# Down projection of a gated hybrid block: difference forms built in the convolution and kept in HBM, six plain groups first, 24 instead of 22 seven-product groups

## The chip, the core and the metric

The kernel runs on one core of a Trainium2 chip. The metric is the device time of one execution in microseconds (us): the median of three runs is 1472.03 us before the change (1471.71, 1472.03 and 1474.16). TensorE (PE) does the matmuls; VectorE (DVE) and ScalarE (ACT) prepare their operands; GpSimd (POOL) and SyncE (SP) here do little but issue DMA transfers.

## The reference

The function is one decoder layer for 256 tokens of width 2048: three kinds of attention, gated and merged, and then a feed-forward part. The change touches only the feed-forward part, which is

```python
h2 = rms_norm(x, g_ffn[l])
u = causal_depthwise_conv(h2 @ w_up[l], conv_w[l], conv_b[l])   # 3 taps, 2 x 5632 channels
u_gate, u_val = jnp.split(u, 2, axis=-1)
x = x + (jax.nn.silu(u_gate) * u_val) @ w_down[l]               # 5632 x 2048
```

Everything is float32 and must come out as precisely as float32 does. The kernel therefore splits every operand into a rounded high part (`hi`, a cast on ACT) and the remainder (`lo`, a subtraction on DVE), and makes three matmuls (hi by hi, lo by hi, hi by lo) where the reference has one product.

## The kernel before, in words

Two stages matter. In the **up projection** (748 to 1241 us of the profiled execution) 11 groups of four column tiles are worked through, each in two halves: the gate columns (`s = 0`) and the value columns (`s = 1`). One half takes eight *ticks*. A tick takes one 512 KB piece of `w_up` (`piece`: load on SP, cast L175 on ACT, subtraction L176 on DVE) and 16 matmuls (eight hi at L1219, eight lo at L1221). The result of a half goes through `conv`, a generator whose pieces are run by `tick()` during the following halves, so its DVE and ACT work is interleaved with the casts and subtractions of the next ticks. After the `s = 1` half, `conv` writes the activation's high and low part for one pair of row tiles into `aT`.

Beside this run the *weight sums* (`weight_sums`, one every seven ticks): the second GEMM uses a Winograd-like scheme in some of its groups, seven block products in place of eight, and needs sums of blocks of `w_down`. Four blocks are loaded into `r0` (one buffer) and `r1` (two buffers) by SP, three or four DVE additions (L1181) make the sums, and POOL stores them to HBM as `T`: one half-megabyte tile (T4 and T2), and a second one (T1 and T3) where four additions were made (`ALL_FOUR`).

The **down projection** (1241 to 1466 us) has 44 groups: 22 pairs of row tiles of `w_down` for each half of the 2048 output columns. `PLANS` sets their order. A plain group (`eight`, "e") has two steps of 12 matmuls. A seven group (`seven`, "s") has four steps of 3, 6, 6 and 6 matmuls, 21 in all; it uses sums of weight blocks against *forms*, that is sums and differences of blocks of the activation. Each step has a preparation, written into the program two steps ahead of its matmuls (`AHEAD = 2`): a load through `buffer`, a ring of four `raw` buffers and, every third turn, two `more` buffers; a cast; a subtraction. The cast and the subtraction write into rings of four `hi` and four `lo` buffers (`SBUFS = 4`). In the seven group, step 0 loads the first row tile, step 1 the second, step 2 the sums T4 and T2, step 3 either loads T1 and T3 or makes them by two DVE additions into a buffer of its own, `t13` (L1371, L1372).

The forms of a pair are made in the down projection by `forms(p)`: five DVE operations on `aT` (L1273 to L1277), two casts on ACT and two subtractions on DVE (L1284, L1285), all in one `fr` buffer.

Every engine, SP included, takes its instructions in program order; `keep` pins that order. A load whose buffer is still being read makes SP wait, and whatever stands behind it in SP's queue waits as well.

## Time and profile before

| what | value | how to read it |
|---|---|---|
| time, median of 3 | 1472.03 us (1471.71 to 1474.16) | device time of a run |
| profiled execution, span | 1469.9 us | first to last instruction; 1.8 us below the fastest run |
| PE busy | 1462.8 us (100%) | the share is rounded; 7.1 us are left |
| DVE / ACT busy | 1205.1 us (82%) / 895.3 us (61%) | |
| up projection, PE / DVE busy | 492.5 / 394.7 of 493.2 us | stage from 748.0 to 1241.2 us |
| down projection, PE / DVE / ACT busy | 224.4 / 208.6 / 140.9 of 224.5 us | stage from 1241.2 to 1465.7 us |
| HBM | 349.70 MB read, 37.75 MB written | |

A row of a timeline reads: start, duration, engine, line, operation, destination<-sources, shapes, and in brackets the idle time ahead of it with what ended it. A row of waits reads: who waited for whom, total, number of waits, longest. The granted TensorE clock is 1.00 in all three stretches of the span (0 to 748, up projection, down projection).

### The profile page before, as it was taken

The numbers are of one execution on the slowest core, as the hardware profiler recorded it, in microseconds if no ns is written. First come the engines' busy times: TensorE is split into PE (matmuls) and PEld (weight loads), VectorE is DVE, ScalarE is ACT, GpSimd is POOL, SyncE is SP. The second block draws the span as 40 slices with busy tenths as digits, with TensorE's granted clock in tenths as the row PEclk, the third lists the DMA queues.
The fourth block names the chain that finished last, engine by engine and source line by source line (L and its number), as shares of the span: only waits on it lengthen the run. The fifth ranks groups of instructions, "written<-read, shape, count | busy, mean of one in ns | idle before, by whom it ended". The sixth has DMA issues, their size and how long they took to land.

```text
span 1469.9 us, 20741 instructions
## 1 busy us (share of the span) xinstructions
PE 1462.8 (100%) x7327; PEld 1233.4 (84%) x7327; DVE 1205.1 (82%) x1617; ACT 895.3 (61%) x1287; POOL 68.8 (5%) x139
## 2 busy tenths in 40 slices
PE   9999999999999999999999999999999999999998
PEld 7888888888878888888888888888888888888887
DVE  5798767766997799888877888788887886998998
ACT  6755454454664466545657667567676777665774
POOL 1000001021000000000000000000000010000000
PEclk9999999999999999999999999999999999999999
DMA  8697898787766576866776888889888895778995
GB/s 295 202 341 260 265 313 270 226 294 267 256 221 204 204 271 247 287 222 237 273 239 218 302 272 276 294 277 310 295 265 273 280 305 190 249 256 286 334 315 191
DMA packets 163463, 388.81 MB, mean 265 GB/s; under 512 B 14016, under 2 KB 22512, under 8 KB 163360
## 3 DMA queue, kind: packets, MB, share of 16 engines
q1 hardware_dynamic: 150960, 345.34, 70.6%
q0 software_dynamic: 11648, 41.10, 7.3%
q8 instruction: 57, 0.93, 0.3%
q10 hardware_dynamic: 752, 1.06, 0.2%
q14 instruction: 46, 0.38, 0.1%
HBM read 349.70 MB, written 37.75 MB: 264 GB/s over the span
## 4 chain that ended last, share of the span: by engine, by line
PE 94%; DVE 3%; DMA 2%; issue 1%; ACT 0%; SPq 0%; DVEq 0%; ACTq 0%
PE u L1219 21%; PE u L1221 10%; PE d L1310 5%; PE d L1309 5%; PE d L1311 5%; PE g_x L769 4%; PE g_x L770 4%; PE g_x L771 4%; PE s L186 2%; PE s L188 2%; PE f L187 2%; PE f L188 2%; PE f L186 2%; PE s L187 2%; PE b L186 2%; PE b L188 2%
## 5 line engine op out<-in xcount | busy, mean ns | idle before, releaser
L1219 PE MATMUL u<-hT,hi_u 128*128 128x512 f32 x1408 | 442.6, 396 | 0.0
L1221 PEld LDWEIGHTS u<-hT,lo_u 128*128 128x128 f32 x1408 | 264.4, 188 | 63.5 <-DVE lo_u L176 1.1
L1221 PE MATMUL u<-hT,lo_u 128*128 128x256 f32 x1408 | 277.0, 278 | 0.7 <-DVE lo_u L176 0.7
L176 DVE TENSOR_TENSOR lo_u<-raw_u,hi_u 128x1024 fp32r<-128x1024 f32 x176 | 213.2, 1220 | 59.8 <-ACT hi_u L175 59.0
L175 ACT CAST hi_u<-raw_u 128x1024 fp32r<-128x1024 f32 x176 | 183.0, 1049 | 107.0 <-PE u L1219 54.6
L1219 PEld LDWEIGHTS u<-hT,hi_u 128*128 128x128 f32 x1408 | 214.5, 189 | 0.1
L764 ACT CAST hi_g<-raw_g 128x1024 fp32r<-128x1024 f32 (+1 forms) x96 | 91.1, 964 | 53.5 <-PE g_x L770 33.4
L765 DVE TENSOR_TENSOR lo_g<-raw_g,hi_g 128x1024 fp32r<-128x1024 f32 (+1 forms) x96 | 105.0, 1116 | 20.9 <-ACT hi_g L764 20.8
L769 PE MATMUL g_x<-hi_g,xT 128*128 128x512 f32 x251 | 98.8, 394 | 0.0
L770 PE MATMUL g_x<-hi_g,xT 128*128 128x512 f32 x251 | 97.7, 389 | 0.0
L771 PE MATMUL g_x<-lo_g,xT 128*128 128x512 f32 x251 | 96.3, 390 | 0.0
L1148 DVE TENSOR_TENSOR y<-y,z 128x512 f32<-128x512 f32 x88 | 60.7, 691 | 24.4 <-ACT z L1147 20.5
L1147 ACT ACTIVATE z<-u,taps 128x256 f32<-128x256 f32 x176 | 74.7, 496 | 0.0
L1309 PE MATMUL d<-hi_d,aT 128*128 128x512 f32 x176 | 68.5, 389 | 0.0
L1310 PE MATMUL d<-hi_d,aT 128*128 128x512 f32 x176 | 68.5, 389 | 0.0
L1311 PE MATMUL d<-lo_d,aT 128*128 128x512 f32 x176 | 68.1, 389 | 0.0
L175 ACT CAST hi_f<-raw_f 128x1024 fp32r<-128x1024 f32 (+1 forms) x40 | 38.6, 968 | 46.6 <-PE f L187 41.9
L186 PE MATMUL s<-hi_s,xT 128*128 128x512 f32 (+1 forms) x160 | 61.9, 387 | 0.0
L175 ACT CAST hi_b<-raw_b 128x1024 fp32r<-128x1024 f32 x32 | 33.6, 1052 | 45.2 <-PE b L187 23.5
L175 ACT CAST hi_s<-raw_s 128x1024 fp32r<-128x1024 f32 (+1 forms) x40 | 38.3, 959 | 36.8 <-PE s L187 29.3
L186 PE MATMUL f<-hi_f,xT 128*128 128x512 f32 (+1 forms) x160 | 60.4, 377 | 0.0
L188 PE MATMUL s<-lo_s,xT 128*128 128x512 f32 (+1 forms) x160 | 59.1, 369 | 0.0
(498 smaller groups left out, 3265.0 us busy)
## 6 DMA issues: line engine op xcount, KB each, us to landing
raw_u<-in_w_up_dram SPq DMA_DIRECT2D x176, 512.0 KB, 5.4
raw_g<-in_w_in_dram SPq DMA_DIRECT2D x86, 512.0 KB, 5.4
T<-r POOLq DMA_DIRECT2D x64, 512.0 KB, 6.1
r<-in_w_down_dram SPq DMA_DIRECT2D x88, 256.0 KB, 5.2
raw_d<-in_w_down_dram SPq DMA_DIRECT2D x44, 512.0 KB, 5.4
raw_f<-in_w_in_dram SPq DMA_DIRECT2D x32, 512.0 KB, 5.5
raw_s<-in_w_in_dram SPq DMA_DIRECT2D x32, 512.0 KB, 5.4
raw_s<-in_w_down_dram SPq DMA_DIRECT2D x32, 512.0 KB, 5.3
```

The lines of the kernel that those rows point to most:

```text
L175: pin(nc.scalar.copy(hi[:, :m], raw[:, :m]))
L176: pin(nc.vector.tensor_tensor(lo[:, :m], raw[:, :m], hi[:, :m].bitcast(F32), ALU.subtract))
L186: nc.tensor.matmul(o, lhsT=xh, rhs=wh, start=first, stop=False)
L188: nc.tensor.matmul(o, lhsT=xh, rhs=wl, start=False, stop=last)
L769: nc.tensor.matmul(o, lhsT=a[0], rhs=w[0], start=first, stop=False)
L770: nc.tensor.matmul(o, lhsT=a[1], rhs=w[0], start=False, stop=False)
L771: nc.tensor.matmul(o, lhsT=a[0], rhs=w[1], start=False, stop=last)
L1219: nc.tensor.matmul(ps, lhsT=hi[:, j, c], rhs=hT[:, k + j, :], start=first, stop=False)
L1221: nc.tensor.matmul(ps[:, :S], lhsT=lo[:, j, c], rhs=hT[:, k + j, :S], start=False, stop=last)
L1309: nc.tensor.matmul(o, lhsT=ah, rhs=w[0], start=first, stop=False)
L1310: nc.tensor.matmul(o, lhsT=al, rhs=w[0], start=False, stop=False)
L1311: nc.tensor.matmul(o, lhsT=ah, rhs=w[1], start=False, stop=last)
```

## The change

Four things change together.

1. **Where the forms are made.** `conv` now calls `unsplit_forms` at the end of the `s = 1` half for the first 14 pairs: three DVE operations on the unsplit activation, written over the tile `y`, and a POOL DMA of 256 KB that stores the four forms to HBM (`rform`, one tensor for two pairs). In the down projection the new `forms(i)` has SP load the forms of two pairs (512 KB) into a tile `fr` with **one** buffer, and later two ACT casts and two DVE subtractions split them. The five DVE operations per pair are gone from the down projection. The loads stand at fixed steps: 6, 10, 16, 24 and 34 of the first column half, and behind two groups of the second.
2. **The plan.** Six plain groups ahead of the first seven group (five before), ten seven groups in the first column half (eight before) and 14 in the second, 24 in all. The kind of each is written into the plan: "t" makes T1 and T3 by additions, "f" loads them. All ten of the first half are "t"; the second half has nine "f" and five "t".
3. **The sums.** 24 weight sums instead of 22: 15 with three additions and nine with four (before, ten and twelve).
4. **Buffers.** `t13` is gone: a "t" group adds in place in the raw buffer of its step 0, an "f" group loads T1 and T3 through the ring. The ring has three `more` buffers, used at three of seven turns (two, at one of three turns, before).

```diff
-PLANS = ("eeeee" + "se" * 5 + "sse" + "s" + "eee", "e" + "sse" * 4 + "ssse" + "sssee")
-ALL_FOUR = {(0, 6), (0, 7)} | {(1, p) for p in range(14) if p not in (4, 6, 8, 11)}
+PLANS = ("eeeeee" + "tte" * 4 + "tt" + "ee", "e" + "ftfe" * 4 + "ft" + "eee")
...
+KINDS = tuple(plan.replace("e", "") for plan in PLANS)
+NFORM = max(NSEVEN)
...
             ended.append(f)
+            if f // 2 < NFORM:
+                yield 1
+                yield from unsplit_forms(f // 2, g, y)
...
+    def unsplit_forms(p, g, y):
+        v = g.rearrange("p k (t q) -> p (k t) q", t=NT)
+        r = y.rearrange("p k (t q) -> p (k t) q", t=NT)
+        tt = nc.vector.tensor_tensor
+        tt(r[:, :2], v[:, 0:4:3], v[:, 1:2].to_broadcast([P, 2, P]), ALU.subtract)
+        yield
+        nc.vector.scalar_tensor_tensor(r[:, FS2], r[:, FS1], -1.0, v[:, 0], ALU.mult, ALU.subtract)
+        tt(r[:, FS4], r[:, FS2], v[:, 2], ALU.add)
+        if p % 2 == 0:
+            rforms[p // 2] = dram.tile([P, 2, 512], F32, name=f"rform{p}")
+        nc.gpsimd.dma_start(rforms[p // 2][:, p % 2], y.rearrange("p k s -> p (k s)"))
...
-        if turn[0] > 10 and turn[0] % 3 == 0:
-            return down_pool().tile([P, PIECE], F32, tag="more", bufs=2, name=name)
+        if turn[0] > 10 and turn[0] % 7 in (1, 3, 5):
+            return down_pool().tile([P, PIECE], F32, tag="more", bufs=3, name=name)
...
+    def forms(i):
+        p = 2 * i
+        n = min(2, NFORM - p)
+        raw = down_pool().tile([P, PIECE], F32, tag="fr", bufs=1, name=f"fr_{i}")[:, : n * 512]
+        keep(nc.sync.dma_start(raw, rforms[i][:, :n].rearrange("p a n -> p (a n)")))
...
+        yield 2
+        keep(nc.scalar.copy(to[:, :, :, 0], r[:, :, :3]))
+        keep(nc.scalar.copy(last[:, :, 0], r[:, :, FS4]))
+        yield
+        keep(nc.vector.tensor_tensor(to[:, :, :, 1], r[:, :, :3], to[:, :, :, 0].bitcast(F32), ALU.subtract))
+        keep(nc.vector.tensor_tensor(last[:, :, 1], r[:, :, FS4], last[:, :, 0].bitcast(F32), ALU.subtract))
...
         def p2():
-            raw[2] = load(made[n0 // PIECE, p][0], f"t{name}")
-            raw[3] = down_pool().tile([P, PIECE], F32, tag="t13", bufs=2, name=f"t13_{name}")
             if four:
-                keep(nc.sync.dma_start(raw[3], made[n0 // PIECE, p][1]))
+                raw[3] = load(made[n0 // PIECE, p][1], f"t13_{name}")
             else:
-                keep(nc.vector.tensor_tensor(raw[3][:, :512], raw[0][:, :512], raw[0][:, 512:], ALU.add))
-                keep(nc.vector.tensor_tensor(raw[3][:, 512:], raw[0][:, 512:], raw[1][:, 512:], ALU.add))
+                add(raw[0][:, :512], raw[0][:, :512], raw[0][:, 512:])
+                add(raw[0][:, 512:], raw[0][:, 512:], raw[1][:, 512:])
+                raw[3] = raw[0]
+            raw[2] = load(made[n0 // PIECE, p][0], f"t42_{name}")
...
         if nb == 0:
             at(-1, lambda: start(0))
+            for i in range(5):
+                at((6, 10, 16, 24, 34)[i], lambda i=i: later(forms(i)))
```

In the program that results, the instructions move at three places of which the prediction speaks. (A row is line, operation, destination<-sources, shape; the numbers in names tell buffers apart.)

SP's queue around the first seven groups, before the change (`raw_d` is a plain group's row tile, `raw_s` a seven group's, `raw_t` the sums):

```order
L1297 DMA raw_d_24_11975<-in_w_down_dram 128x1024
L1297 DMA raw_d_25_12005<-in_w_down_dram 128x1024
L1297 DMA raw_s_0_12033<-in_w_down_dram 128x1024
L1297 DMA raw_s_1_12060<-in_w_down_dram 128x1024
L1297 DMA raw_t_0_12080<-T_0_0_7283 128x1024
L1297 DMA raw_d_26_12104<-in_w_down_dram 128x1024
```

and now:

```order
L1289 DMA raw_d_31_12120<-in_w_down_dram 128x1024
L1289 DMA raw_s_0_12140<-in_w_down_dram 128x1024
L1297 DMA fr_12160<-rform_7902 128x1024
L1289 DMA raw_s_1_12162<-in_w_down_dram 128x1024
L1289 DMA raw_t_0_0_12182<-T_0_0_7283 128x1024
L1289 DMA raw_s_2_12203<-in_w_down_dram 128x1024
L1289 DMA raw_s_3_12217<-in_w_down_dram 128x1024
L1289 DMA raw_t_0_1_12231<-T_0_1_7495 128x1024
L1297 DMA fr_12240<-rform_8362 128x1024
L1289 DMA raw_d_32_12252<-in_w_down_dram 128x1024
```

The load of the second pair of forms (`fr_12160`) stands between the loads of the first seven group's two row tiles (steps 12 and 13), and that of the third (`fr_12240`) ahead of the next plain group's (step 20). The next one (`fr_12349`) stands in the same way ahead of `raw_s_7`, the load of step 27.

DVE's order at the same place, now:

```order
L1314 TENSOR_TENSOR lo_s_0_12143<-raw_s_0_12140,hi_s_0_12142 128x512
L1305 TENSOR_TENSOR sf<-fr_12074,sf 128x6x128
L1306 TENSOR_TENSOR aT<-fr_12074,aT 128x2x128
L1314 TENSOR_TENSOR lo_s_1_12165<-raw_s_1_12162,hi_s_1_12164 128x1024
L1364 TENSOR_TENSOR raw_s_0_12140<-raw_s_0_12140 128x512
L1364 TENSOR_TENSOR raw_s_0_12140<-raw_s_0_12140,raw_s_1_12162 128x512
L1314 TENSOR_TENSOR lo_t_0_0_12185<-raw_t_0_0_12182,hi_t_0_0_12184 128x1024
L1314 TENSOR_TENSOR lo_t_0_0_12192<-raw_s_0_12140,hi_t_0_0_12191 128x1024
L1314 TENSOR_TENSOR lo_s_2_12206<-raw_s_2_12203,hi_s_2_12205 128x512
L1305 TENSOR_TENSOR sf<-fr_12160,sf 128x6x128
L1306 TENSOR_TENSOR aT<-fr_12160,aT 128x2x128
L1314 TENSOR_TENSOR lo_s_3_12220<-raw_s_3_12217,hi_s_3_12219 128x1024
```

The two subtractions that read the first `fr` tile, and so free its one buffer for `fr_12160`, come behind the subtraction of step 12; those that free it for `fr_12240` come behind that of step 16 (`lo_s_2`), and, further on, those for `fr_12349` behind that of step 22 (`lo_s_4`).

DVE's order in the up projection between two subtractions of `w_up` pieces (ticks 20 to 22), before:

```order
L176 TENSOR_TENSOR lo_u_0_8_7441<-raw_u_0_8_7439,hi_u_0_8_7440 128x1024
L1163 TENSOR_TENSOR aT<-y_0_7117,aT 128x2x256
L1181 TENSOR_TENSOR r_0_1_7307<-r_0_1_7307 128x512
L1148 TENSOR_TENSOR y_1_7357<-y_1_7357,z_2_1_7360 128x512
L176 TENSOR_TENSOR lo_u_0_10_7464<-raw_u_0_10_7462,hi_u_0_10_7463 128x1024
...
L1181 TENSOR_TENSOR r_0_1_7308<-r_0_1_7308 128x512
L176 TENSOR_TENSOR lo_u_0_12_7489<-raw_u_0_12_7487,hi_u_0_12_7488 128x1024
L1163 TENSOR_TENSOR aT<-y_0_7133,aT 128x2x256
```

and now:

```order
L1177 TENSOR_TENSOR y_1_7339<-y_0_7117 128x256
L177 TENSOR_TENSOR lo_u_0_8_7450<-raw_u_0_8_7448,hi_u_0_8_7449 128x1024
L1164 TENSOR_TENSOR aT<-y_0_7117,aT 128x2x256
L1179 SCALAR_TENSOR_TENSOR y_1_7339<-y_1_7339,y_0_7117 128x128
...
L1180 TENSOR_TENSOR y_1_7339<-y_1_7339,y_0_7117 128x128
...
L1177 TENSOR_TENSOR y_1_7357<-y_0_7133 128x256
L1164 TENSOR_TENSOR aT<-y_0_7133,aT 128x2x256
L1179 SCALAR_TENSOR_TENSOR y_1_7357<-y_1_7357,y_0_7133 128x128
L1200 TENSOR_TENSOR r_0_1_7308<-r_0_1_7308 128x512
L1180 TENSOR_TENSOR y_1_7357<-y_1_7357,y_0_7133 128x128
L177 TENSOR_TENSOR lo_u_0_12_7498<-raw_u_0_12_7496,hi_u_0_12_7497 128x1024
```

Ahead of tick 22's subtraction (`lo_u_0_12`) there now stand six operations more that make forms (L1177, L1179 and L1180, for each of two pairs) and the subtraction into `aT` (L1163 before, L1164 now) that came behind it.

More of the change, by code (lines that the diff above doesn't have):

```diff
@@ L49 @@
 OUT_SEVENS = 3
-NSEVEN = tuple(plan.count("s") for plan in PLANS)
+KINDS = tuple(plan.replace("e", "") for plan in PLANS)
+NSEVEN = tuple(len(kinds) for kinds in KINDS)
+NFORM = max(NSEVEN)
 @with_exitstack
@@ L1164, in conv @@
             ended.append(f)
+            if f // 2 < NFORM:
+                yield 1
+                yield from unsplit_forms(f // 2, g, y)
+    FS3, FS1, FS2, FS4 = range(4)
+    rforms = {}
+    def unsplit_forms(p, g, y):
[9 more added lines that the diff above has]
+        nc.gpsimd.dma_start(rforms[p // 2][:, p % 2], y.rearrange("p k s -> p (k s)"))
     ended = []
     made = {}
-    asked = [(0, p) for p in range(NSEVEN[0])] + [(1, p) for p in range(NSEVEN[1])]
+    asked = [(nb, p) for nb in range(2) for p in range(NSEVEN[nb])]
     def weight_sums(nb, p):
@@ L1181, in weight_sums @@
         add = lambda o, i: tc.keep_in_program_order(nc.vector.tensor_tensor(o, o, i, ALU.add))
-        four = (nb, p) in ALL_FOUR
+        four = KINDS[nb][p] == "f"
         add(r[0][:, 0], r[0][:, 1])
@@ L1246, in hybrid_block @@
     ov = out[0].rearrange("(t p) d -> p t d", p=P)
-    FS3, FS1, FS2, FS4 = range(4)
     sf = xt_pool.tile([P, 10, 3, 2, P], F32R, tag="xt", name="sf")
@@ L1258, in form_of @@
             return pieces_of(p)[:, 0, :, 1]
[L1259 to L1285 removed]
+        return sf[:, p % 10, f]
     turn = [0]
@@ L1298, in load @@
         return raw
+    def forms(i):
[3 more added lines that the diff above has]
+        keep(nc.sync.dma_start(raw, rforms[i][:, :n].rearrange("p a n -> p (a n)")))
+        r = raw.rearrange("p (a f q) -> p a f q", a=2, f=4)[:, :n]
+        to = sf[:, p % 10 : p % 10 + n]
+        last = aT[:, 2 * p : 2 * (p + n)].rearrange("p (a k) (l t q) -> p a k l t q", k=2, l=2, t=NT)[:, :, 0, :, 1]
+        yield 2
[4 more added lines that the diff above has]
+        keep(nc.vector.tensor_tensor(last[:, :, 1], r[:, :, FS4], last[:, :, 0].bitcast(F32), ALU.subtract))
+        issued.update((f"forms{p}", f"forms{p + 1}"))
     def parts(src, name):
@@ L1353, in seven @@
         w, raw = {}, {}
-        four = (n0 // PIECE, p) in ALL_FOUR
+        four = KINDS[n0 // PIECE][p] == "f"
+        add = lambda o, a, b: keep(nc.vector.tensor_tensor(o, a, b, ALU.add))
         def p0():
@@ L1381, in u1 @@
         def u1():
+            assert f"forms{p}" in issued
             three(X()[0][0], *a_of(k1, 0), w["10"])
@@ L1445, in results @@
                     (nc.scalar if nb else nc.gpsimd).dma_start(ov[:, t, xc], xr)
-    formed = 0
     after_step = {}
@@ L1454, in hybrid_block @@
         n0 = nb * PIECE
-        ns, s = plan.count("s"), 0
+        ns, s = NSEVEN[nb], 0
         X, Y = (lambda nb=nb: banks[nb][0]), (lambda nb=nb: banks[nb][1])
@@ L1460, in hybrid_block @@
             at(-1, lambda: start(0))
+            for i in range(5):
+                at((6, 10, 16, 24, 34)[i], lambda i=i: later(forms(i)))
         for i, c in enumerate(plan):
-            if c == "s":
+            if c != "e":
                 seven(s, n0, X, Y, s == 0, s == ns - 1)
+                if nb and s % 2 and s // 2 + 5 < (NFORM + 1) // 2:
+                    at(len(steps), lambda i=s // 2 + 5: later(forms(i)))
                 s += 1
@@ L1471, in hybrid_block @@
                     at(len(steps) - 1, lambda nb=nb: residual(nb))
-                if formed < ns and n_done >= 4 - 3 * nb:
-                    at(len(steps) - 2, lambda p=formed: later(forms(p)))
-                    formed += 1
-        assert s == ns and not straight and formed >= ns
+        assert s == ns and not straight
         at(len(steps) - 1, finish)
```

25 lines of the change are left out of this document (removed).

## The prediction

> **What bounds the kernel now.** I read the page's head and its chain of waits first: who is on the path that sets the end, and how much of the span is not that.
>
> ```profile
> span 1469.9 us, 20741 instructions
> PE 1462.8 (100%) x7327; PEld 1233.4 (84%) x7327; DVE 1205.1 (82%) x1617; ACT 895.3 (61%) x1287; POOL 68.8 (5%) x139
> PE 94%; DVE 3%; DMA 2%; issue 1%; ACT 0%; SPq 0%; DVEq 0%; ACTq 0%
> ```
>
> PE is busy for 1462.8 of 1469.9 us. Only 7.1 us are not matmuls, 4.2 of them behind 1465.7, where the second stretch shown next ends. So a change can win hardly more than the matmuls it takes away, and any lateness of an operand is paid in full. Next the stretches of the two stages (columns: time, then busy us and instructions of PE, PEld, DVE, ACT, POOL; clock; DMA share; GB/s), then the matmuls' line in the second one, and PE's waits.
>
> ```profile
> 748.00:1241.20 493.20, 492.52 (x2834) 429.58 (x2834) 394.74 (x482) 343.05 (x534) 21.05 (x40) 1.00 0.83 275
> 1241.20:1465.70 224.50, 224.44 (x991) 185.54 (x989) 208.58 (x286) 140.88 (x174) 4.33 (x8) 1.00 0.78 270
> 1241.20:1465.70 224.50, 128.23 (x330) 61.77 (x329) 1.00 0.78 270
> PE u L1221 <- DVE lo_u L176: 0.7, 1, 0.7
> ```
>
> PE never stops in the down projection, and once, for 0.7 us, in the up projection. One of the three matmuls of a product stands 330 times, so there are 990, at 224.44 / 990 = 0.2267 us each. DVE is busy for 208.6 of 224.5 us: it follows closely, and what matters is by how much each `lo` tile is ahead of PE (its lead).
>
> **Matmuls removed.** 24 seven groups instead of 22 take away 2 x 3 matmuls: 6 x 0.2267 = **-1.4 us**, all on the path.
>
> **The forms in the down projection.** Before, these rows belonged to them (busy us, mean ns):
>
> ```profile
> L1273 DVE TENSOR_TENSOR fd<-aT 128x512 f32<-128x512 f32 x14 | 9.6, 684 | 0.0
> L1275 DVE TENSOR_TENSOR fr<-fd 128x256 f32<-128x256 f32 x14 | 5.9, 418 | 0.0
> L1276 DVE SCALAR_TENSOR_TENSOR fr<-fr,rbc 128x128 f32<-128x128 f32 x14 | 4.1, 292 | 0.5
> L1277 DVE TENSOR_TENSOR fr<-fr,rbc 128x128 f32<-128x128 f32 x14 | 4.1, 292 | 0.5
> L1284 DVE TENSOR_TENSOR sf<-fr,sf 128x384 fp32r<-128x384 f32 x10 | 5.5, 550 | 0.0
> L1285 DVE TENSOR_TENSOR aT<-fr,aT 128x128 fp32r<-128x128 f32 x14 | 4.0, 283 | 0.0
> ```
>
> With L1274, which has L1275's shape, the five operations that go are 9.6 + 2 x 5.9 + 2 x 4.1 = 29.6 us of DVE. The subtractions stay, for two pairs at once: 768 and 256 elements. Between the rows of 256 and 512 elements lie 684 - 418 = 266 ns, so 768 take some 0.95 us, and with 0.42 and 0.1 of overlap a double is 1.27 us. DVE thus gets some 20 us less to do in the down projection, but it isn't PE, and PE waited for nothing there: the relief is worth **0**. What is new is a load in SP's queue that waits for DVE. Here is the first seven group of before around steps 10 and 11, which the changed plan has at steps 12 and 13 in the same surroundings (plain groups ahead, a group with additions):
>
> ```profile
> 1253.79 0.80 SPq L1297 DMA_DIRECT2D raw_s<-in_w_down_dram  x2
> 1260.79 0.69 DVE L1305 TENSOR_TENSOR lo_s<-raw_s,hi_s 128x512 fp32r<-128x512 f32 x1 [0.49 <-ACT hi_s L1304]
> 1262.85 1.05 ACT L1304 CAST hi_s<-raw_s 128x1024 fp32r<-128x1024 f32 x1 [2.10 <-PE d L1310]
> 1263.99 1.22 DVE L1305 TENSOR_TENSOR lo_s<-raw_s,hi_s 128x1024 fp32r<-128x1024 f32 x1
> 1265.13 0.68 DVE L1371 TENSOR_TENSOR t<-raw_s 128x512 f32<-128x512 f32 x1
> 1265.73 0.69 DVE L1372 TENSOR_TENSOR t<-raw_s,raw_s 128x512 f32<-128x512 f32 x1
> 1266.90 0.38 SPq L1297 DMA_DIRECT2D raw_t<-T  x1
> 1269.41 0.39 PE L1311 MATMUL d<-lo_s,aT 128*128 128x512 f32 x1
> ```
>
> Both row tiles were asked for by 1254.6; the second one's `lo` was done at 1263.99 + 1.22 = 1265.21, 4.2 us before PE read it (1269.41). Now the load of the second pair of forms stands between the two. It has one buffer, so SP issues it only when the subtractions of the first forms are done, and these follow step 12's subtraction on DVE. Behind SP wait the loads of step 13, of T4 and T2, and of the next group. How long such a load takes (median us from issue to landing), in the whole stage, and, in the last row, alone:
>
> ```profile
> raw_s<-in_w_down_dram SPq DMA_DIRECT2D x32, 512.0 KB, 5.3
> t<-T SPq DMA_DIRECT2D x12, 512.0 KB, 6.6
> raw_d<-in_w_down_dram SPq DMA_DIRECT2D x2, 512.0 KB, 3.7
> ```
>
> From the end of step 12's subtraction (1261.48 in the model) to PE's need there are 1269.41 - 1261.48 = 7.9 us. The chain in it: subtractions of the forms 1.3, issue of the forms' load 0.4, load of step 13 5.3, cast 1.05, subtraction 1.2, together 9.3. **First stall +1.4 us** (with a load of 3.7, 0; with 6.6, 2.7). I take 5.3, because the forms' load of the same size runs beside it.
>
> The Trainium skill, "DMA: Bandwidth & Descriptors", section "Anatomy of one DMA — SWDGE (gpsimd) path", fits a transfer on another issue path as 2.0 us and its bytes over 436 GB/s, by estimate 3.2 us for 512 KB; by it this first term would be 0, which is the first rival's side. This trace agrees only roughly, with 3.7 us for a pair by itself, and the same section's remark that the wait for a semaphore lies with the issuing sequencer is how SP's rows read here.
>
> From then on step 13's `lo` has no lead, and DVE has its own backlog up to the last `lo` of the second group: twice two additions (0.60 apart by the rows above), five subtractions of 1024 (1.14 apart: 1.22 less an overlap of 0.08), one of 512 (0.6) and the forms' double (1.3), in all 2.4 + 5.7 + 0.6 + 1.3 = 10.0 us. PE has 33 matmuls there, 7.5 us. **Second stall +2.4 us** (2.2 if the first load is quick; it doesn't start from a shortage otherwise).
>
> The third forms' load stands ahead of step 20's. It waits for the second forms' subtractions, behind step 16's. From that point DVE and PE come to step 20 in 1.3 + 1.14 + 1.2 + 2 x 1.14 = 5.9 us and six matmuls, 1.4: 7.3 us. The chain through SP takes 9.3: **+2.0 us** (0.4 to 3.3). The fourth stands ahead of step 27 and waits for step 22's subtraction. Between lie 24 matmuls, 5.4 us, and some 2.5 us of lead that the plain group has given back (its 24 matmuls take 5.4 us, its two subtractions 2.3), 7.9 in all, again against 9.3: **+1.2 us**, rounded down for what the earlier stall leaves in the ring (0 to 2.5). The later forms' loads find their buffer free. A plain group and two with additions ask 14.0 us of DVE (with one double) and 15.0 of PE, so leads grow by only 1 us in each three groups; I charge nothing more. Down projection: 1.4 + 2.4 + 2.0 + 1.2 = **+7.0 us** (2.6 to 10.9).
>
> The additions in place hold a raw buffer for two steps more, which the third `more` buffer is to make good; T1 and T3 are loaded 9 times instead of 12. I set these at 0; the bound is a further ring wait like the above, within the 10.9. Seven loads of forms add 3.7 MB to a stage with a DMA share of 0.78: also 0.
>
> **The forms in the up projection.** Three operations per pair, 0.42 + 0.29 + 0.29 less three overlaps, are 0.76 us, for two pairs 1.5 us in each of seven halves. Where DVE has slack this is free. The first such half falls on the tightest place of the stage:
>
> ```profile
> 801.53 0.68 DVE L1137 TENSOR_TENSOR cr<-cr,u 128x512 f32<-128x512 f32 x1
> 809.82 1.22 DVE L176 TENSOR_TENSOR lo_u<-raw_u,hi_u 128x1024 fp32r<-128x1024 f32 x1
> 810.95 0.68 DVE L1163 TENSOR_TENSOR aT<-y,aT 128x512 fp32r<-128x512 f32 x1
> 811.42 0.40 PE L1221 MATMUL u<-hT,lo_u 128*128 128x256 f32 x2
> ```
>
> DVE runs without a pause from 801.53, and tick 22's `lo_u` is done at 811.04, 0.38 us before PE reads it. Now the 1.5 us and L1163's 0.6 stand ahead of it: 2.1 - 0.38 = **+1.7 us** (1.1 if the moved subtraction is absorbed, 2.2 with no overlap). Against it stands the stall of 0.7 us that the page shows. These rows tell its cause:
>
> ```profile
> SPq L1177 <- DMA T<-r: 48.9, 17, 5.7
> 963.08 0.53 POOL L1191 DMA_DIRECT2D T<-r  x1 [17.51 <-DVE r L1181]
> 968.70 0.91 SPq L1177 DMA_DIRECT2D r<-in_w_down_dram  x2
> 969.72 1.55 SPq L172 DMA_DIRECT2D raw_u<-in_w_up_dram  x3
> ```
>
> The load of the next sum's `r0` waited for the store of T1 and T3 out of the one `r0` buffer, and three loads of `w_up` stood behind it. The sum that made this store (the tenth) now has three additions and no such store: **-0.7 us**. The other six halves keep 1.5 us more on DVE; one of them is close:
>
> ```profile
> 1018.00:1040.00 22.00, 22.00 (x129) 19.20 (x128) 20.82 (x27) 15.23 (x25) 1.09 (x3) 1.00 0.89 299
> 973.00:995.00 22.00, 21.32 (x122) 18.27 (x122) 17.57 (x24) 13.89 (x23) 1.06 (x2) 1.00 0.92 309
> ```
>
> 20.82 + 1.5 is 22.3 us in 22.0, a loss that leads of a few us carry. Up projection: **+1.0 us** (0.4 to 2.5).
>
> **The sum.** -1.4 + 1.0 + 7.0 = +6.6 us: the profiled execution from 1469.9 to 1476.5, the median, which lies 2.1 us above that execution, from 1472.03 to **1478.6 us**; own range -1.4 + 0.4 + 2.6 to -1.4 + 2.5 + 10.9, that is 1473.6 to 1484.0. About 0.2%, 2.9 us, can be told from no change in this kernel.
>
> **Rivals.**
>
> *Loads in time, not slower.* If the loads behind SP's wait take the 3.7 us of the lone pair, step 13 is in time, and if DVE, relieved of 20 us, enters the seven groups with a lead that outlasts the 10.0 against 7.5 us, only the matmuls and perhaps the 0.7 us count: 1472.03 - 1.4 - 0.7 + 0 to 1.7 = 1470 to 1471.6. It decides at a load of 3.9 us for step 13 (7.9 - 4.0 for the rest of the chain). For it: DVE's busy time drops. Against it: that load runs beside another, and the median is 5.3.
>
> *The up projection becomes bound by DVE.* If each of the other six halves loses its 1.5 us as the first does, 9 us come on top: 1487.6. For it: the 20.82 us above. Against it: 17.57 in the other row, and DVE's own waits in this stage, which are for ACT's casts, 59.0 of 59.8 us:
>
> ```profile
> L176 DVE TENSOR_TENSOR lo_u<-raw_u,hi_u 128x1024 fp32r<-128x1024 f32 x176 | 213.2, 1220 | 59.8 <-ACT hi_u L175 59.0
> ```
>
> *The clock.* If a stall of over 3 us makes the throttle lower the clock, matmuls take longer for some time after. The row of 973 to 995 us shows a clock of 1.00 through a stall of 0.7 us; longer ones don't occur here. Were the clock halved for as long as the seven groups' backlog, 33 matmuls, 7.5 us more: 1486. The Trainium skill, "TensorE: Matmul & The Clock Gate", section "Part 1: The HAM clock gate", has half the clock behind an idle window of about 3.4 us. None of my single stalls is as long, so this hangs on two that join.
>
> *The change doesn't do what it says:* a forms' load that waits for its store. The stores lie hundreds of us earlier; I give it nothing.
>
> **Chances.** Forecast 0.57, loads in time 0.28, DVE-bound up projection 0.10, clock 0.05. The second is within 0.2%, and so is a little of the first (its lower end): same 0.32. Faster by 2.9 us is more than the 1.4 + 0.7 that can be won, so only the measurement leaves 0.03. Slower is the rest, 0.65. The range takes in the first two cases, and not the last two: 1470.0 to 1484.
>
> **What would show it.** PE's waits: one at tick 22 of the up projection on `lo_u`, of 1.7 us, and none on tick 85; in the down projection three or four, on `lo_s` or `lo_t` of the first two seven groups, on the `lo_d` of step 20 and on step 27. In SP's waits the forms' load waiting for its own subtractions for several us, four times. 984 matmuls. DVE in the down projection at some 189 us. Wrong would be: step 13's `lo` done 2 us or more ahead of PE; no idle time of PE behind step 12; a pause at other halves of the up projection.

## The result, and the profile after

The changed kernel takes 1487.51 us (median of four runs, 1485.33 to 1488.57), the kernel before 1472.24 us beside it: a ratio of 1.0102, 95% interval 1.0087 to 1.0116. It is slower by 15.3 us, where 6.6 were forecast, and lies above the range (1470.0 to 1484.0).

The head of the page after, its chain of waits, and all that PE waited for from the up projection on (who waited for whom, total us, times, longest):

```profile
span 1486.9 us, 20757 instructions
PE 1470.9 (99%) x7321; PEld 1231.7 (83%) x7321; DVE 1201.6 (81%) x1592; ACT 894.1 (60%) x1277; POOL 76.0 (5%) x152
PE 87%; DMA 5%; DVE 5%; ACT 2%; issue 1%; SPq 0%; DVEq 0%; ACTq 0%
```

```profile
PE d L1318 <- ACT hi_s L1313: 2.8, 2, 2.5
PE d L1318 <- ACT hi_t L1313: 1.9, 3, 1.1
PE d L1318 <- ACT hi_d L1313: 1.1, 1, 1.1
PE d L1320 <- DVE lo_s L1314: 1.1, 2, 0.5
PE d L1320 <- DVE lo_t L1314: 0.7, 2, 0.5
PE u L1240 <- DVE lo_u L177: 0.6, 1, 0.6
```

Before, the chain was PE for 94% and the down projection had no row among these waits. Now it has five. There are six matmuls fewer and PE is busy for longer (1470.9 against 1462.8 us): some matmuls took more time (5.4 of these 8.1 us lie in the down projection, the rest ahead of the up projection). The stretches of the two stages begin and end in the trace with these matmuls:

```profile
1244.83 0.40 PE L1240 MATMUL u<-hT,lo_u 128*128 128x256 f32 x2
1245.06 0.40 PE L1318 MATMUL d<-hi_d,aT 128*128 128x512 f32 x1
...
1482.55 0.39 PE L1320 MATMUL d<-lo_d,aT 128*128 128x512 f32 x1
```

From the start of its first to the start of its last matmul the down projection takes 237.49 us; the 983 distances between its 984 matmuls would take 222.80 at the pitch of the kernel before (0.2267 us, taken here as 0.22665). I call the difference, 14.69 us, its *lateness*; before, it was 0.04 us of 224.20. The up projection takes 493.38 us (493.44 before). The rest is ahead of both: the up projection starts at 751.68 in this execution and at 747.60 in the one of before, though the program is the same up to there; the fourteen profiled executions behind this document (these two, and one of each kernel below) start it between 747.35 and 751.68, and 3.0 of the 4.1 us between these two were lost in the first 27 us of the program. So of the 17.0 us between the two spans 13.3 are the down projection's and 4.1 the start's; the medians differ by 15.3, and the two us of it that aren't the down projection's are in reach of what the start differs by.

Where the 14.69 us lie, step by step (summed from the starts of the matmuls, against 0.22665 us each):

| place | forecast, us | measured, us |
|---|---|---|
| steps 13 and 14, first seven group | 1.4 | 5.2 |
| steps 18 and 19, DVE's backlog | 2.4 | 1.8 |
| step 20, load behind the third forms' load | 2.0 | 1.8 |
| steps 27 to 29, load behind the fourth | 1.2 | 2.4 |
| all behind step 29 | 0 | 3.5 |

The first of these in the trace. SP's queue, DVE, ACT and PE of the changed kernel around steps 12 and 13:

```profile
1259.53 0.33 SPq L1289 DMA_DIRECT2D raw_s<-in_w_down_dram  x1
1272.16 0.33 SPq L1297 DMA_DIRECT2D fr<-rform  x1
1272.54 0.69 SPq L1289 DMA_DIRECT2D raw_s<-in_w_down_dram  x1
1273.28 0.42 SPq L1289 DMA_DIRECT2D raw_t<-T  x1
1273.74 0.90 SPq L1289 DMA_DIRECT2D raw_s<-in_w_down_dram  x2
1274.69 0.65 SPq L1289 DMA_DIRECT2D raw_t<-T  x1
```

```profile
1270.20 0.69 DVE L1314 TENSOR_TENSOR lo_s<-raw_s,hi_s 128x512 fp32r<-128x512 f32 x1 [1.07 <-ACT hi_s L1313]
1270.81 0.95 DVE L1305 TENSOR_TENSOR sf<-fr,sf 128x768 fp32r<-128x768 f32 x1
1271.68 0.42 DVE L1306 TENSOR_TENSOR aT<-fr,aT 128x256 fp32r<-128x256 f32 x1
1281.10 1.23 DVE L1314 TENSOR_TENSOR lo_s<-raw_s,hi_s 128x1024 fp32r<-128x1024 f32 x1 [9.00 <-ACT hi_s L1313]
```

```profile
raw_s<-in_w_down_dram SPq DMA_DIRECT2D x1, 512.0 KB, 7.4
```

```profile
1278.18 0.39 PE L1320 MATMUL d<-lo_s,aT 128*128 128x512 f32 x1
1281.12 0.50 PE L1318 MATMUL d<-hi_s,aT 128*128 128x512 f32 x1 [2.54 <-ACT hi_s L1313]
1282.38 0.69 PE L1320 MATMUL d<-lo_s,aT 128*128 128x512 f32 x1 [0.53 <-DVE lo_s L1314]
1282.86 0.63 PE L1318 MATMUL d<-hi_s,aT 128*128 128x512 f32 x1
1283.29 0.63 PE L1319 MATMUL d<-hi_s,aT 128*128 128x512 f32 x1
```

SP issues nothing from 1259.86 to 1272.16, until the two subtractions of the first forms are done; DVE then idles for 9.00 us, because step 13's row tile, asked for at 1272.54, takes 7.4 us. PE stops for 2.5 us. And behind the stop the matmuls start 0.43 us apart, not 0.23: the clock was lowered. In three stretches of 2 us (columns: time; busy us and instructions of PE, PEld, DVE, ACT, POOL; clock; DMA share; GB/s):

```profile
1282.00:1284.00 2.00, 1.62 (x4) 1.35 (x5) 1.97 (x4) 0.80 (x2) 0.00 (x0) 0.63 0.59 240
1284.00:1286.00 2.00, 2.00 (x6) 1.54 (x6) 1.94 (x2) 2.00 (x4) 0.00 (x0) 0.52 0.06 23
1286.00:1288.00 2.00, 2.00 (x11) 1.60 (x10) 1.67 (x4) 2.00 (x3) 0.00 (x0) 1.00 0.00 0
```

### The profile page after: what moved, and what is told of

Same layout as the page of the kernel before. It is cut to its first block, busy times and chain, and to the rows that moved or that the text cites. A ratio compares the mean times of both kernels' runs of the same rounds, so it can differ in the third digit from the quotient of the medians.

```text
span 1486.9 us, 20757 instructions
## 1 busy us (share of the span) xinstructions
PE 1470.9 (99%) x7321; PEld 1231.7 (83%) x7321; DVE 1201.6 (81%) x1592; ACT 894.1 (60%) x1277; POOL 76.0 (5%) x152
## 4 chain that ended last, share of the span: by engine, by line
PE 87%; DMA 5%; DVE 5%; ACT 2%; issue 1%; SPq 0%; DVEq 0%; ACTq 0%
PE u L1238 21%; PE u L1240 10%; PE d L1320 4%; PE d L1318 4%; PE d L1319 4%; PE g_x L770 4%; PE g_x L771 4%; PE g_x L772 4%; PE f L187 2%; PE f L188 2%; PE f L189 2%; PE b L189 2%; PE b L187 2%; PE b L188 2%; PE s L189 2%; PE s L187 2%
## 5 line engine op out<-in xcount | busy, mean ns | idle before, releaser
L1318 PE MATMUL d<-hi_d,aT 128*128 128x512 f32 x160 | 62.5, 391 | 1.2 <-ACT hi_d L1313 1.1
L1319 PE MATMUL d<-hi_d,aT 128*128 128x512 f32 x160 | 62.3, 389 | 0.0
L1320 PE MATMUL d<-lo_d,aT 128*128 128x512 f32 x160 | 61.3, 391 | 0.1
L1314 DVE TENSOR_TENSOR lo_d<-raw_d,hi_d 128x1024 fp32r<-128x1024 f32 x40 | 48.3, 1221 | 14.0 <-ACT hi_d L1313 13.3
```

The source lines that it names most:

```text
L1318: nc.tensor.matmul(o, lhsT=ah, rhs=w[0], start=first, stop=False)
L1319: nc.tensor.matmul(o, lhsT=al, rhs=w[0], start=False, stop=False)
L1320: nc.tensor.matmul(o, lhsT=ah, rhs=w[1], start=False, stop=last)
```

## The experiments

The theory: nearly all of the lateness is SP standing behind a forms' load that waits for its one buffer. Rivals: the ring of buffers without `t13`; DVE's backlog in two groups with additions in a row, or the dense plan altogether; forms that come late. The table has all runs; lateness and the stages are from the profiled execution of each, the time and the ratio from its runs against those of the kernel before on the same chip. Lateness is thus that of one execution, and of one that can lie 3 us above the median of its kernel; the time is the surer number.

| kernel | time, us | ratio to before (95%) | up, us | lateness in down, us |
|---|---|---|---|---|
| before | 1472.24 | | 493.44 | 0.04 |
| changed | 1487.51 | 1.0087 to 1.0116 | 493.38 | 14.69 |
| forms' loads at later steps | 1478.83 | 1.0034 to 1.0059 | 494.87 | 8.39 |
| forms' loads on POOL | 1478.72 | 1.0028 to 1.0056 | 494.12 | 6.65 |
| second forms' load a step later | 1486.14 | 1.0080 to 1.0116 | 494.82 | 14.17 |
| second forms' load alone on POOL | 1482.17 | 1.0049 to 1.0083 | 492.79 | 10.78 |
| two small forms' buffers on SP | 1474.26 | 1.0010 to 1.0028 | 493.42 | 4.09 |
| POOL, T4 and T2 loaded first | 1474.09 | 1.0006 to 1.0025 | 493.44 | 5.18 |
| small buffers, T4 and T2 first, forms later in the convolution | 1471.20 | 0.9994 to 1.0011 | 492.49 | 1.41 |
| POOL, old plan (990 matmuls) | 1477.54 | 1.0030 to 1.0060 | 498.20 | 1.47 |
| the same, first ten sums without second store | 1475.05 | 1.0015 to 1.0037 | 494.91 | 1.56 |
| POOL, t13 and ring as before | 1482.95 | 1.0066 to 1.0096 | 493.44 | 12.88 |
| forms made in the down projection | 1494.36 | 1.0141 to 1.0171 | 492.50 | 25.17 |
| before, forms also made and stored | 1477.18 | 1.0020 to 1.0044 | 497.20 | 0.02 |

**Is it SP's queue?** First the places of the loads, and their queue.

```diff
-                at((6, 10, 16, 24, 34)[i], lambda i=i: later(forms(i)))
+                at((6, 14, 24, 34, 44)[i], lambda i=i: later(forms(i)))
```

> The changed kernel with the loads of the forms at steps 6, 14, 24, 34 and 44 of the first column half in place of 6, 10, 16, 24 and 34, so that each finds the subtractions of the forms before it done. My theory: of the 14.7 us that PE loses in the down projection of the changed kernel nearly all comes from SP standing behind a forms' load that waits for its one buffer; without that wait PE loses under 2 us there, and with 6 matmuls less the time is 1470.5 us, 1469.5 to 1472.5. Rival A, the ring (raw buffers held by the additions in place, other turns, more bytes): the stalls stay, 1484 to 1488. Rival B, DVE's backlog in two groups with additions in a row: the 2.4 us per such pair stay in the first one at least, 1474 to 1478.

Measured: 1478.83 us. Lateness falls from 14.69 to 8.39, not to 2. Up to step 29 only 0.6 us are left of 11.2, so the four stalls are gone from their places, but SP still waits for the forms' subtractions for 20.1 us in all:

```profile
SPq L1297 <- DVE aT L1306: 20.1, 5, 7.2
```

In the changed kernel that row reads 38.1 us:

```profile
SPq L1297 <- DVE aT L1306: 38.1, 5, 12.9
```

At the second forms' load SP was some seven steps ahead of DVE, so ten steps between two forms' loads are not enough for one buffer. I took the wait as gone when it was only halved; but that isn't why the time missed my 1470.5. Of the 8.39 us 7.8 lie behind step 29, where I had expected nothing, and the next kernel, in which SP doesn't wait for the forms at all, takes the same time.

```diff
-        keep(nc.sync.dma_start(raw, rforms[i][:, :n].rearrange("p a n -> p (a n)")))
+        keep(nc.gpsimd.dma_start(raw, rforms[i][:, :n].rearrange("p a n -> p (a n)")))
```

> The changed kernel with the loads of the forms issued by POOL and not by SP, at the same places and with the same one buffer: the forms come as late as in the changed kernel and the wait for the buffer stays, but nothing stands behind it. My theory: the four stalls go, 1470.5 us (1469.5 to 1473). Rival A (ring) and a rival C, that the forms themselves come late: 1484 to 1488.

Measured: 1478.72 us, lateness 6.65. The same loads wait for the same buffer, but on POOL's queue, behind which nothing stands, and 8.0 us of lateness are gone. Up to step 29 0.8 us of the 11.2 are left. So the wait in SP's queue is the cause of the stalls there, and forms that come late (rival C) are not. The size I expected was wrong again: 3.9 us appear at steps 75 to 77.

```diff
-                at((6, 10, 16, 24, 34)[i], lambda i=i: later(forms(i)))
+                at((6, 11, 16, 24, 34)[i], lambda i=i: later(forms(i)))
```

> The changed kernel with the second forms' load one step later (11 for 10), behind the load of step 13 and still ahead of the load of T4 and T2 (step 14). My theory: step 13 has no stall, the wait now falls on step 14, whose load is issued at the same 12 us after the ring had room, but is needed 6 matmuls (1.4 us) later and has one transfer less beside it: 5.2 us of lateness at steps 13 and 14, half clock in it, become 1 to 2.5, the later stalls stay; 1483 to 1485 us. If SP's place isn't the cause, 1487.5.

Measured: 1486.14 us, above the 1483 to 1485 expected. Step 13 has no stall, as expected, and step 14 none either; the lateness comes back at step 18 (1.9 us) and 20 (4.4 us, with seven matmuls 0.43 us apart). A step's difference moves the stall; lateness is 0.5 us less.

```diff
-        keep(nc.sync.dma_start(raw, rforms[i][:, :n].rearrange("p a n -> p (a n)")))
+        keep((nc.gpsimd if i == 1 else nc.sync).dma_start(raw, rforms[i][:, :n].rearrange("p a n -> p (a n)")))
```

> The changed kernel with the second forms' load alone (the one between the loads of steps 12 and 13) issued by POOL; the others stay on SP. It prices the first wait by itself. In the changed kernel PE lost 5.2 us at steps 13 and 14, 1.4 of it as matmuls at half clock behind the gap. Theory: these 5.2 us go, and of the 1.8 at steps 18 and 19, which were DVE's backlog behind the first stall, 0.6 stay as with all forms' loads on POOL; the waits ahead of steps 20 and 27 remain with their 1.8 and 2.4 us or a little less: 6 us less, 1480.5 to 1482.5. If the later stalls only follow from the first, 1478.7 as with all of them on POOL.

Measured: 1482.17 us. Steps 13 and 14 lose nothing, 18 and 19 1.0 us, step 20 1.9 and steps 27 to 29 2.4, as in the changed kernel. The 5.2 us of the first wait are gone, and the stalls at steps 20 and 27 don't follow from it; of the 1.8 us at steps 18 and 19 0.8 did. In all lateness falls by 3.9 us only, since 5.4 us and not 3.5 are lost behind step 29, at places like those of the kernel with POOL; the time falls by 5.3.

**Is it SP, or the one buffer?** The forms of one pair per load, two buffers in the same room, loads behind both groups of a round and not between them:

```diff
-        raw = down_pool().tile([P, PIECE], F32, tag="fr", bufs=1, name=f"fr_{i}")[:, : n * 512]
-        keep(nc.sync.dma_start(raw, rforms[i][:, :n].rearrange("p a n -> p (a n)")))
+        raw = down_pool().tile([P, 512], F32, tag="fr", bufs=2, name=f"fr_{p}")
+        keep(nc.sync.dma_start(raw, rforms[p // 2][:, p % 2]))
...
-                at((6, 10, 16, 24, 34)[i], lambda i=i: later(forms(i)))
+                at((6, 6, 16, 16, 26, 26, 36, 36, 46, 46)[p], lambda p=p: later(forms(p)))
```

> The changed kernel with the forms' loads still on SP, but one pair each (256 KB) into two buffers, which take the same room as the one of 512 KB, and two at a time at steps 6, 16, 26, 36 and 46, behind both groups of a round and not between them. If only the wait for the one buffer in SP's queue made the 8 us that the forms' loads on POOL took away, SP does as well as POOL: SP waits for the forms' subtractions under 10 us in all (38.1 in the changed kernel) and the time is 1478 to 1480 us, as with POOL. If SP's place costs in itself (bytes, order), 1483 to 1487.

Measured: 1474.26 us, 4 us under my expectation and better than with POOL. SP's wait for the forms' subtractions is 12.8 us, a little over the 10 expected, in shorter pieces:

```profile
SPq L1295 <- DVE aT L1304: 12.8, 8, 4.8
```

Up to step 63 lateness is 0.1 us with all ten groups with additions of the first column half. So neither SP, nor the bytes, nor DVE's work there costs anything in this arrangement, and rival B falls as a cause of its own: DVE's work with two such groups in a row costs at most 0.7 us at steps 18 and 19 with POOL, and nothing here. Two things changed together, the buffers and the steps of the loads; which of them does it, and why it is better than POOL, isn't shown.

**The rest behind step 64.** The next two kernels, and the fourth from here, start from the one with all forms' loads on POOL (the two with the old plan issue them at steps 6, 12, 22, 32 and 42). There, at steps 75 to 77 (the third group of the second half, which loads T1 and T3), SP asks for T1 and T3 ahead of T4 and T2, which are needed a step earlier; output rows and the residual's rows of the other half move then too. SP's loads of the sums, with the next issue behind them, and PE at that place:

```profile
1366.67 0.96 SPq L1289 DMA_DIRECT2D raw_t<-T  x2
1372.47 0.81 SPq L1289 DMA_DIRECT2D raw_d<-in_w_down_dram  x2
```

```profile
1376.07 0.40 PE L1320 MATMUL d<-lo_s,aT 128*128 128x512 f32 x1
1378.13 0.51 PE L1318 MATMUL d<-hi_t,sf 128*128 128x512 f32 x1 [1.66 <-ACT hi_t L1313]
1378.46 0.60 PE L1319 MATMUL d<-hi_t,sf 128*128 128x512 f32 x1
1380.00:1382.00 2.00, 2.00 (x6) 1.52 (x6) 2.00 (x3) 1.53 (x2) 0.00 (x0) 0.53 0.80 295
```

(The last row is a stretch, with the clock in its third column from the end: 0.53. Some 1.6 of the 3.9 us are matmuls that started 0.40 to 0.43 us apart.)

```diff
-            if four:
-                raw[3] = load(made[n0 // PIECE, p][1], f"t13_{name}")
-            else:
+            if not four:
...
             raw[2] = load(made[n0 // PIECE, p][0], f"t42_{name}")
+            if four:
+                raw[3] = load(made[n0 // PIECE, p][1], f"t13_{name}")
```

> The changed kernel with the forms' loads on POOL, and in the groups that load T1 and T3 the load of T4 and T2 (needed a step earlier) issued ahead of that of T1 and T3, as in the kernel before. With the forms' loads on POOL alone, PE still lost 6.65 us in the down projection, 3.9 of them in one such group at steps 75 to 77, where T4 and T2 landed 7 us after the row tiles. If the order of the two loads is the cause there: 2 to 3 us less, 1476 us. If it is the load on the transfers at the change of column halves: 1478 to 1479.

Measured: 1474.09 us. Steps 75 to 77 lose 1.5 us and not 3.9; 5.18 us of lateness are left in all, the rest in pieces of at most 0.9 us. These steps alone don't show it: in the six other kernels with the old order of the two loads and the dense plan, the changed one among them, they lose 0.8 to 2.8 us. The times do: 2.5 us above the kernel before, and 6.0 without the new order, with intervals that don't meet.

```diff
-PLANS = ("eeeeee" + "tte" * 4 + "tt" + "ee", "e" + "ftfe" * 4 + "ft" + "eee")
+PLANS = ("eeeee" + "te" * 5 + "tfe" + "f" + "eee", "e" + "ffe" * 2 + "tfe" * 2 + "tffe" + "tffee")
```

> The changed kernel with the forms' loads on POOL (at steps 6, 12, 22, 32 and 42) and with the order of groups, the kinds and the 22 seven groups of the kernel before: 990 matmuls, forms from HBM, the new ring, additions in place. If the remaining 6.65 us come from the denser plan, PE loses under 1.5 us in the down projection (225.7 us from its first to its last matmul) and the time is 1473 to 1475 us. If they come from the ring and the place of T1 and T3 in it, 4 to 7 us stay: 1478 to 1481.

Measured: lateness 1.47 us, as expected if the plan is the cause. But the time is 1477.54 us, since the up projection now takes 498.20, 4.8 more than before. The kernel before, with the forms' additions and stores put in, shows the same:

```diff
             ended.append(f)
+            if f // 2 < max(NSEVEN):
+                yield 1
+                yield from unsplit_forms(f // 2, g, y)
```

> The kernel before with the forms made in the convolution as well and stored to HBM, but not read; the down projection makes its own as before. It prices the part of the change in the up projection alone. From the changed kernel, where PE waited once there, 0.8 us at tick 22, and the old wait of 0.7 us was gone with its store: here both stay, +0.8 us, 1472.2 to 1473.5. A DVE-bound up projection would give +5 to +9.

Measured: 1477.18 us, the up projection 497.20, +3.8 and not +0.8. PE's waits there, and SP at the later of the two places:

```profile
PE u L1239 <- DVE lo_u L176: 2.6, 2, 1.9
```

```profile
969.69 0.37 SPq L172 DMA_DIRECT2D raw_u<-in_w_up_dram  x1
972.29 0.94 SPq L1195 DMA_DIRECT2D r<-in_w_down_dram  x2
973.34 2.07 SPq L172 DMA_DIRECT2D raw_u<-in_w_up_dram  x3
```

It is the old place, where the load of `r0` waits for the store out of it; the wait of 0.7 us has become 1.9. Which of the two makes it, the additions or the second store? The old plan with its first ten sums of three additions:

```diff
-PLANS = ("eeeee" + "te" * 5 + "tfe" + "f" + "eee", "e" + "ffe" * 2 + "tfe" * 2 + "tffe" + "tffee")
+PLANS = ("eeeee" + "te" * 5 + "tte" + "t" + "eee", "e" + "tte" + "ffe" + "tfe" * 2 + "tffe" + "tffee")
```

> The kernel with the old order of groups and forms from HBM by POOL, with one thing changed: the first ten sums (all eight of the first column half and two of the second) have three additions and no second store, as in the changed kernel; before, the sums 7 to 10 had four. In that kernel PE took 498.2 us for the up projection, 4.8 more than before, with 4.5 us of waits at four places, one of them (2.3 us) where the old wait of 0.7 stood. If the second stores, which hold the one r0 buffer, are what makes the forms' additions cost so much there: up projection 493.5 to 494.5, time 1473 to 1474.5 us (1477.5 without). If the additions alone do it: 497 to 498, 1477.

Measured: 1475.05 us, the up projection 494.91 (498.20 without): the later wait is gone, waits at ticks 21 and 22 stay, as in some executions of the changed kernel's convolution. So the changed kernel's kinds, ten "t" first, save its convolution from 3.3 us; the forms' additions alone don't cost them, but with sums of four additions at that place they do. Such a sum has a second store and also one addition more on DVE, which this run doesn't separate; that the `r0` load waits for this store is what the trace of the kernel above shows (the store lands at 972.27 us, the load is issued at 972.29). Time and up projection came out a little above what I expected.

**Are the ring and the lighter DVE needed?** First, on the kernel with POOL, the buffers as before (and the forms one pair per load, for room):

```diff
-        if turn[0] > 10 and turn[0] % 7 in (1, 3, 5):
-            return down_pool().tile([P, PIECE], F32, tag="more", bufs=3, name=name)
+        if turn[0] > 10 and turn[0] % 3 == 0:
+            return down_pool().tile([P, PIECE], F32, tag="more", bufs=2, name=name)
...
+            raw[3] = down_pool().tile([P, PIECE], F32, tag="t13", bufs=2, name=f"t13_{name}")
```

> The changed kernel with the forms' loads on POOL, one pair each (256 KB, steps 6, 11, 15, 20 and so on, so that the smaller tile leaves room), and with the buffers of the kernel before: two t13 buffers of their own, T4 and T2 loaded first, two more buffers at every third turn. 984 matmuls, plan and forms as changed. If the ring is the cause of the remaining 6.65 us: under 1.5 of them stay, 1472 to 1474 us. If it is the plan: 1477 to 1479.

Measured: 1482.95 us, 12.88 us of lateness, outside both of my expectations. The old ring isn't the cure: with it lateness is 6.2 us more than with the new one under this plan. PE waits for DVE in ten places, six of them on the sums:

```profile
PE d L1318 <- DVE lo_t L1312: 3.8, 6, 0.7
PE d L1318 <- DVE lo_s L1312: 2.5, 3, 0.8
```

SP's longest waits there are for the additions that free a row tile's buffer:

```profile
SPq L1289 <- DVE t L1362: 72.8, 15, 6.4
```

That the ring's smaller depth makes the loads late in this way is an argument; no experiment took it apart, and the forms' loads also stood at other steps here.

Then, on the changed kernel, the forms back in the down projection:

```diff
-            if f // 2 < NFORM:
-                yield 1
-                yield from unsplit_forms(f // 2, g, y)
...
+    def forms(i):
+        for p in range(2 * i, min(2 * i + 2, NFORM)):
+            yield from forms_of(p)
```

(`forms_of` is the old `forms`, five DVE operations on `aT`.)

> The changed kernel with the forms made in the down projection as before (five DVE operations per pair, nothing stored or read in HBM), in the places of the changed kernel; plan, ring and sums as changed. Theory: no load of forms blocks SP, and the up projection is as before or better (its 0.7 us wait gone). But a plain group and two with additions now ask 18.6 us of DVE in 15.0 of PE, so DVE sets the pace in the first column half: 4.5 such rounds times 3.6, less some 5 us of lead, +11, 1482 to 1488 us. If DVE's relief is worth nothing, as I had it: 1476 to 1479.

Measured: 1494.36 us, the slowest. DVE is busy for 61.6 of the 66 us of three rounds, PE waits for it, and the clock falls to 0.90 on average:

```profile
1267.00:1333.00 66.00, 56.97 (x216) 43.67 (x215) 61.60 (x103) 33.67 (x47) 0.00 (x0) 0.90 0.59 196
```

So with this ring and these places the dense plan can't be had without the forms moved.

**All together.** Two small buffers on SP, T4 and T2 first, and the forms four ticks later in the convolution:

```diff
             if f // 2 < NFORM:
-                yield 1
+                yield 5
```

> Two changes on the kernel with two small forms' buffers on SP: the load of T4 and T2 ahead of that of T1 and T3, and the forms in the convolution four ticks later, so that they stand behind tick 22's subtraction. PE's wait at tick 22 (0.8 us in the changed kernel) should be gone, the up projection at 492.6 to 492.9 us, the down projection at 228 us as with that order of loads on POOL: 1473 to 1474 us, within 0.2% of the kernel before. To beat it the dense plan's remaining 5 us would have to go too, which nothing here does.

Measured: 1471.20 us (11 runs) beside 1471.11 us (23 runs of before), ratio 1.0003, 0.9994 to 1.0011. PE's waits from the up projection on:

```profile
PE d L1318 <- DVE lo_t L1312: 0.2, 1, 0.2
PE d L1316 <- DVE e L1427: 0.2, 1, 0.2
```

The up projection takes 492.49 us, 1.0 less than before, without a wait at tick 22; but the kernel with the second forms' load alone on POOL, whose forms stand where the changed kernel has them, has no wait there either in its profiled execution, so that the later place took it away isn't shown. The down projection takes 224.21 us, as long as before: lateness is 1.41 us, which eats up the six matmuls. Against the kernel with two small buffers, 2.7 us of lateness went; of the two edits between them the order of the loads is the one in the down projection. (This profiled execution took 1470.39 us, the shortest of its runs, and the other's 1475.94, the longest of its runs; by the medians 3.1 us went, up projection included.) My expectation that the dense plan itself would keep 5 us was wrong: most of them went with the buffers and the order of the loads. No kernel here beats the one before; the best one equals it within 0.1%.

## Why the prediction was right or wrong

*What bounds the kernel, and the matmuls.* Right: PE had nothing to give, 984 matmuls at the same pitch save 1.4 us, and every late operand was paid in full.

*The mechanism in SP's queue.* Right in kind and place: stalls at steps 13, 20 and 27, made by a forms' load that waits for its one buffer, and one at steps 18 and 19 from DVE's backlog. With these loads on POOL 10.4 of the 11.2 us up to step 29 go, and 8.0 us in all. "The later forms' loads find their buffer free" was wrong for the fifth, which waited for 3.7 us.

*First stall, +1.4.* Wrong in size; this step failed most. It cost 5.2 us. The chain was right but for one term: the load of step 13, for which I took the median of 5.3 us because one other load ran beside it, took 7.4. By the trace: 1.2 us of subtractions, SP 0.4, the load 7.4, cast 1.05, subtraction 1.2 and 0.2 between them are 11.5 us in 8.0, so 3.5 late. The upper bound I had formed (6.6 us, 2.7 late) was too low as well. The other 1.7 us are eight matmuls started 0.43 to 0.49 us apart in place of 0.23. Of the 7.7 us by which the lateness is above the 7.0 forecast, this step made 3.8, what lies behind step 29 3.5 and steps 27 to 29 1.2; steps 18 to 20 took 0.8 less than forecast.

Why this load took 7.4 us stays open. When SP was let go, it issued six transfers within 2.5 us, and my own sentence on what stood behind the wait had named them. But the row tiles of steps 20 and 27, let go behind a forms' load in the same way (with five and four transfers issued together), took:

```profile
raw_d<-in_w_down_dram SPq DMA_DIRECT2D x1, 512.0 KB, 5.6
raw_s<-in_w_down_dram SPq DMA_DIRECT2D x1, 512.0 KB, 5.4
```

In the kernel with the second forms' load a step later, six were issued within 2.5 us at step 20, and the first row tile took 5.8. So the number of transfers doesn't explain it. The stall itself is hardly an accident of one execution: with this one forms' load on POOL the median fell by 5.3 us, as much as it cost.

*The clock.* I had it as a rival with a chance of 0.05, only where two stalls join. Stops of 2.5 and 0.5 us, with two matmuls between them, were enough. The Trainium skill, "TensorE: Matmul & The Clock Gate", section "Part 1: The HAM clock gate", gives an idle window of about 3.4 us for half the clock, by which this stall would have cost nothing beyond itself; the granted clock of 0.52 behind it says otherwise, though its size, one half, agrees.

*DVE's backlog, +2.4, and step 20, +2.0.* Both about right (1.8 and 1.8), step 20 with a load of 5.6 us where I had 5.3. The backlog follows from the first stall only in part: 1.0 us stay when that stall alone is taken away, 0.7 with all forms' loads on POOL, none with two small buffers.

*Step 27, +1.2.* Step 27 itself lost 1.3 us, with a load of 5.4: right. What I left out are the 1.0 us at steps 28 and 29. They are DVE's additions once more: the cast of T1 and T3 could start only behind them, and PE, which had lost its lead, read its result at 1311.08 us.

```profile
1309.18 0.69 DVE L1364 TENSOR_TENSOR raw_s<-raw_s,raw_s 128x512 f32<-128x512 f32 x1
1309.98 1.05 ACT L1313 CAST hi_t<-raw_s 128x1024 fp32r<-128x1024 f32 x1 [1.36 <-DVE raw_s L1364]
```

*"I charge nothing more".* Wrong by 3.5 us: 1.5 in the rest of the first column half, 2.0 in the second. The first 1.5 fall to 0.6 with the forms' loads on POOL and to 0.1 with the small buffers. In the second half, that T1 and T3 are asked for ahead of T4 and T2, which I set at 0 with the ring, costs 1.5 us (loads on POOL) to 2.7 us (small buffers) of lateness in those kernels; how much of the 2.0 it makes in the changed one no run shows. The bound I left for the ring, "within the 10.9", didn't hold: 14.69 us were lost.

*The forms' relief is worth 0.* Right for the plan of before, where the down projection lost nothing, wrong as a statement on the change: under the new plan, with the forms back in the down projection, lateness is 25.17 us and not 14.69. DVE is busy for 193.7 us in the changed kernel's down projection, where I had some 189 (208.6 before).

*Up projection, +1.0.* Measured -0.1 here; the kernels with the same program there lie between 492.79 and 494.87, with waits at ticks 21 and 22 of nothing to 1.8 us in all. In the changed kernel the wait at tick 22 came (0.6 us, forecast 1.7), and the one of tick 85 is gone as forecast. What I missed is that, without the new kinds, the old wait would have grown to 1.9 us.

*The rivals and the range.* "Loads in time" lost at its own point, a load of 3.9 us. A DVE-bound up projection didn't come. The range ended at 1484.0, because its upper end let the load take 6.6 us at most, and had nothing for the clock and nothing for what lies behind step 29.

## What to carry to other kernels

A load that waits for a buffer stops the whole queue behind it, and what stands behind it pays a whole load's time, for which a median is no bound: here it was 7.4 us where the median was 5.3. Two buffers of half the size in the same room (with the loads at other steps), or the same load on a queue behind which nothing waits, took most of that away without another byte of memory; the order in which two loads of one step are issued was worth as much as the matmuls saved. Where PE is busy all the time, as here, a plan with fewer matmuls pays only if every lead survives it, and a stop of 2.5 us had a lowered clock's price of 1.7 us on top.

## What the runs showed of the hardware

The lowered clock came behind shorter stops than I expected. Behind stops of about 2.5 us (step 13 of the changed kernel, with one of 0.5 us right after it, and step 20 of the one with the second load a step later) seven matmuls each started 0.43 us apart; behind one of 1.66 us that followed smaller ones (steps 75 and 76 of the kernel with POOL) seven did as well. In the kernel with later forms' loads, matmuls that started 1.5, 1.9 and 1.7 us behind the one before had no such run behind them. Where the edge lies these runs don't tell.

Six transfers of 512 KB issued within 2.5 us (steps 13 and on of the changed kernel) landed after 3.2, 7.4 and up to 10.5 us. While the second was under way, from 1275 to 1280 us, 209 to 295 GB/s were moved; in the two us behind it, from 1280 to 1282 us, it was 397, at a DMA share of 1.00. Such row tiles had a median of 5.3 us in the steady stage of before.

The start of the program differs from one execution to the next by up to 4.3 us at the up projection's first matmul, with the same instructions (granted clock over its first 27 us: 1.00 in the execution of before and 0.94 in that of the changed kernel); two single executions of such kernels can't be compared by their spans, only stage by stage.
